# First layer's gathers ordered behind each V block, and the second layer's context projected last

## The chip, the cores and the metric

The kernel runs on one core of one Trainium2 chip. The metric is the device time of one execution in microseconds (us), taken from the first to the last instruction with what lies around them; lower is better. The engines are named as in the profile: PE multiplies matrices, DVE works element by element on tensors, ACT does activations, casts and copies, POOL writes the descriptors of indirect DMAs (the gathers), and SP issues all other DMAs.

## The reference

Two layers over 512 latent tokens (x) and 256 context tokens, 1024 wide, all in float32. Each layer mixes tokens by three head groups and then looks up experts:

```
hx = rmsnorm(x) * (1 + sc1) + sh1                       # the same for the context, hc
ux, uc = split(hx @ w_in), split(hc @ w_in)             # 18 slices of 128 columns
A: conv width 4 -> RG-LRU scan both ways; the context's last state starts x's scan
B: latent attention: x attends to context and x
C: hyena: conv width 3, two long convolutions by FFT
x = x + g1 * (concat(A * gelu, B, C) @ w_out)
hx = rmsnorm(x) * (1 + sc2) + sh2
# PEER: 8 heads, top 16 of 128 x 128 experts: 128 experts a token
x = x + g2 * sum(gate * gelu(hx . u_tab[eid]) * v_tab[eid])
```

The context gets an output of its own only in the first layer. In the second it gives keys, values and the LRU's starting state, so just six of its 18 slices are needed: 0 to 2 (LRU input), 9 and 10 (compressed keys and values) and 11 (rotary key).

## The kernel before, in words

Instructions are written in one stream with a priority for each part (`self.prio(n)`, lower goes first). A scheduler fixes the order of every engine when the program is built, from these priorities and from its own durations. Nothing is reordered at run time: an engine that waits holds up all that stands behind it.

**Experts, first layer.** 384 of the 512 tokens of x are done densely in `peer_x` (L1180): for each of 128 blocks of 128 experts a U block (weights from DRAM, tile `uv`, split into a high half `uvh` on ACT and a low half `uvl` on DVE, then matmuls into `pst`) and a V block (the same split, matmuls into `dacc`). Between them stands `weights` (L1236): it turns the routed gates into dense columns PA and PB by one-hot tiles (`o`, `og`, matmuls `pwt`). This is done in three groups of blocks, 36, 46 and 46 wide; R = 64 U blocks are held at once. The loop over m at L1305 to L1316 writes, for each m, the weights that are due, V block m and U block m + 64.

The last 128 tokens of x and the 256 of the context are done by gathers: 128 indirect DMAs for u and 128 for v per tile of 128 tokens, each one expert row per token (512 KB into one of 5 buffers `grow`), and one DVE multiply-add each (`acc`, L1134 for u, L1147 for v). `gtile_u` and `gtile_v` write them. Before, all of them have priority 6, the dense loop 3, the second layer's front 3 and 4: the scheduler places a gather where it finds DVE free.

**Second layer's front.** `front` norms and transposes x (`ptr`, `hraw`, `hT`), multiplies it by the slices of `w_in` (each split into `w_inh` on ACT and `w_inl` on DVE; matmuls `pwin`), then does hyena (`hpf`, `hpo`), then `lru` for the context (gates `lpg`, `lg`, `lA`, `lT` from `cxx`) and for x (from `xx`) and the keys and values (`bps`). The slices go 12 to 17 (hyena's), 3 to 8, and then the shared ones 9, 10, 11, 0, 1, 2, whose split weights are used for x and for the context (`cT`). `back` loads and splits the eight slices of `w_out` (L577 to L586): five early, three late, and multiplies (`pwo`).

Of the kernel before, what the change touches and what calls it, by code (L numbers as in the profile page):

```python
# [2 lines left out]

# [17 lines left out]
D = 1024  # L21
# [50 lines left out]
class Kern:  # L72
# [101 lines left out]
    def schedule(self):  # L174
        a = self.a
        with ExitStack() as er:
# [28 lines left out]
            with self.prio(6):  # L205
                self.gtile_u(0, gc[0])
                self.gtile_v(0, 1, 0, gc[0])
                self.gtile_u(0, gc[1])
            with self.prio(3):
                gx, ex = self.peer_x(0, 384, 6, 31, 33, (36, 46, 46), ex, rn)  # L210
# [12 lines left out]
            with self.prio(5):  # L223
                gx, _ = self.peer_x(1, 320, 0, 32, 46, (44, 42, 42), (ex,))
            with self.prio(6):
                for i in sorted(gx, reverse=True):
                    self.gtile_u(1, gx[i])
                    self.gtile_v(1, 0, i, gx[i])
# [235 lines left out]
    def front(self, es, ps, pr, l, s, low, side="left", split=True, ctx=False):  # L464
# [26 lines left out]
        with ExitStack() as es2:  # L491
            hp = es2.enter_context(self.pool("hyc" + tg, side=side))
            hc = [hp.tile([128, L], F32, name=f"hc_{i}") for i in range(6)]
            with self.pool("win" + tg, side=side) as sp:

                def post(st, L, j, p):
                    if j < 3:
                        u = sp.tile([128, LX + 3], F32, name="upad", bufs=2)
                        nc.gpsimd.memset(u[:, 0:2], 0.0)
                        nc.gpsimd.memset(u[:, L + 2:L + 3], 0.0)  # L500
                        nc.scalar.copy(u[:, 2:L + 2], p)
                        cw = [self.col(l, "lcw", i * 3 + j) for i in range(4)]
                        self.conv(st["xx"][j], u, L, cw, self.col(l, "lcb", j))
                    elif j < 6:
                        nc.scalar.activation(st["u1"][j - 3], p, AF.Gelu_apprx_tanh)
                    elif j < 9:
                        nc.scalar.copy(st["cq"][j - 6], p)
                    elif j < 11:
                        nc.scalar.copy(st["ckv"][j - 9], p)
                    elif j == 11:  # L510
                        nc.scalar.copy(st["kr"], p[:96])
                    else:
                        u = sp.tile([128, LX + 3], F32, name="upad", bufs=2)
                        nc.gpsimd.memset(u[:, 0:1], 0.0)
                        nc.gpsimd.memset(u[:, L + 1:L + 2], 0.0)
                        nc.scalar.copy(u[:, 1:L + 1], p)
                        cw = [self.col(l, "hcw", i * 6 + j - 12) for i in range(3)]
                        self.conv(hc[j - 12], u, L, cw, self.col(l, "hcb", j - 12))

                def parts(name, L):  # L520
                    return [sp.tile([128, KD, L], F32R if split else F32, name=f"{name}{i}") for i in range(1 + split)]

                hT = parts("hT", L)
# [614 lines left out]
    def gtile_v(self, l, s, t, routed):  # L1138
# [25 lines left out]
        if l == 0:  # L1164
            nc.sync.dma_start(self.sd[s][t], res)
            if s == 0:
                nc.sync.dma_start(self.res[0][:, t, :], self.sd[0][t])
# [298 lines left out]
```

## Time and profile before

| | |
|---|---|
| median of 3 runs | 4270.21 us (4254.28 to 4272.61) |
| profiled execution | 4259.61 us, span 4257.7 us |
| granted PE clock, mean | 0.939 of full |
| busy: PE, DVE, ACT, POOL | 87%, 82%, 45%, 36% |
| dense loop of the first layer, V blocks | 1207.6 to 2456.6 us |
| second layer up to x's first gate | 2456.6 to 2694.05 us |

Busy shares are means over stages with different limits. To see what a moved instruction costs one reads the stage it leaves and the stage it enters: which engine is full there, and which wait ends last. A group's "idle before" is the time for which its engine stood still just ahead of it, and the releaser is what ended that.

### The profile page before, as it was taken

How to read it: one execution, taken by the hardware profiler on the slowest of the kernel's cores; microseconds unless marked ns; L12 is line 12 of the kernel's file. 1: busy time of each engine (PE TensorE's matmuls, PEld its weight loads, DVE VectorE, ACT ScalarE, POOL GpSimd, SP SyncE). 2: the span in 40 equal slices, each digit the busy share in tenths (PEclk: the TensorE clock that was granted, in tenths of full speed). 3: DMA queues.
4: the chain of work that ended last, by engine and by line, in shares of the span. 5: the costliest groups of instructions: out<-in, count | busy, mean ns of one | idle time of the engine just before them, and what ended most of it. 6: DMA issues, size and time to landing. Idle time of an engine off the chain costs nothing.

```text
span 4257.7 us, 63783 instructions
## 1 busy us (share of the span) xinstructions
PE 3709.5 (87%) x22514; PEld 2804.8 (66%) x22514; DVE 3508.1 (82%) x7449; ACT 1902.7 (45%) x3719; POOL 1524.0 (36%) x1225
## 2 busy tenths in 40 slices
PE   6887988967989999988968979888888999999997
PEld 3645544557878878877756656447888877776654
DVE  5746988889899989988898875754898988898988
ACT  4555243523247426622552244633334755555732
POOL 0000345642344564366436620000126345553243
PEclk7998998979989999999989989998999999999999
DMA  6655687885768897799879952242359888888697
GB/s 204 203 178 183 214 307 244 300 288 185 250 226 266 307 363 268 243 361 348 292 233 332 348 181 87 84 142 100 138 180 352 270 296 296 294 299 277 227 352 274
DMA packets 305634, 1063.74 MB, mean 250 GB/s; under 512 B 35756, under 2 KB 42624, under 8 KB 305314
## 3 DMA queue, kind: packets, MB, share of 16 engines
q0 software_dynamic: 165888, 604.05, 40.8%
q1 hardware_dynamic: 139426, 455.61, 30.7%
q8 instruction: 177, 2.90, 0.3%
q14 instruction: 143, 1.17, 0.1%
HBM read 1042.69 MB, written 16.84 MB: 249 GB/s over the span
## 4 chain that ended last, share of the span: by engine, by line
PE 32%; DMA 21%; DVE 19%; issue 16%; POOL 6%; ACT 5%; SPq 0%; POOLq 0%; DVEq 0%; ACTq 0%
PE pst L121 7%; POOL grow L1123 6%; PE dacc L121 6%; DMA grow<-in_peer_u_dram,eid 6%; DMA grow<-in_peer_v_dram,eid 5%; DMA uv<-in_peer_v_dram 4%; PE pwin L121 4%; DMA uv<-in_peer_ut_dram 3%; DVE uvl L114 3%; DVE acc L1147 3%; DVE acc L1134 2%; PE ppq L121 2%; DMA wmod<-in_w_mod_dram 2%; PE pwo L121 1%; PE fp L414 1%
## 5 line engine op out<-in xcount | busy, mean ns | idle before, releaser
L1123 POOL DMA_INDIRECT grow<-in_peer_u_dram,eid x576 | 749.6, 1301 | 1166.6 <-DVE acc L1134 591.8
L1123 POOL DMA_INDIRECT grow<-in_peer_v_dram,eid x576 | 766.8, 1331 | 748.0 <-DVE acc L1147 604.4
L121 PE MATMUL pst<-dhT,uvh 128*128 128x384 f32 (+1 forms) x4096 | 998.6, 328 | 0.0
L113 ACT CAST uvh<-uv 128x1024 fp32r<-128x1024 f32 x491 | 512.9, 1045 | 699.7 <-DMA uv<-in_peer_v_dram 422.4
L121 PE MATMUL pst<-dhT,uvl 128*128 128x384 f32 (+1 forms) x2048 | 695.2, 339 | 115.5 <-DVE uvl L114 83.9
L1147 DVE SCALAR_TENSOR_TENSOR acc<-grow,gate,acc 128x1024 f32<-128x1024 f32 x571 | 732.9, 1283 | 49.9 <-DMA grow<-in_peer_v_dram,eid 42.9
L1134 DVE SCALAR_TENSOR_TENSOR acc<-grow,ghx 128x1024 f32<-128x1024 f32 x576 | 704.4, 1223 | 73.4 <-DMA grow<-in_peer_u_dram,eid 68.4
L121 PEld LDWEIGHTS pst<-dhT,uvh 128*128 128x128 f32 x4096 | 730.6, 192 | 2.8 <-issue 1.2
L114 DVE TENSOR_TENSOR uvl<-uv,uvh 128x1024 fp32r<-128x1024 f32 x491 | 599.5, 1222 | 154.8 <-ACT uvh L113 152.1
L121 PEld LDWEIGHTS pst<-dhT,uvl 128*128 128x128 f32 x2048 | 394.2, 192 | 218.2 <-DVE uvl L114 163.5
L121 PE MATMUL dacc<-uvh,wl 128*128 128x512 f32 x1154 | 482.0, 418 | 40.1 <-ACT uvh L113 21.3
L121 PE MATMUL dacc<-uvl,wh 128*128 128x512 f32 x1154 | 468.8, 406 | 25.7 <-DVE uvl L114 25.4
L121 PE MATMUL dacc<-uvh,wh 128*128 128x512 f32 x1154 | 462.9, 401 | 0.0
L1263 ACT ACTIVATE o<-iota,di2n 128x128 f16<-128x128 f16 x1056 | 325.2, 389 | 27.6 <-PE pwt L1267 27.4
L121 PEld LDWEIGHTS dacc<-uvh,wl 128*128 128x128 f32 x1154 | 220.6, 191 | 130.3 <-ACT uvh L113 37.0
L121 PEld LDWEIGHTS dacc<-uvl,wh 128*128 128x128 f32 x1154 | 221.1, 192 | 84.5 <-DVE uvl L114 40.2
L121 PEld LDWEIGHTS dacc<-uvh,wh 128*128 128x128 f32 x1154 | 221.2, 192 | 47.9
L1267 PEld LDWEIGHTS <-o 128*128 128x128 f16 x4224 | 126.4, 97 | 104.3 <-issue 31.1
L1233 ACT ACTIVATE PA<-pst 128x320 f32<-128x320 f32 (+1 forms) x126 | 58.4, 463 | 290.4 <-PE pst L121 290.3
L1267 PE MATMUL pwt<-og,o 128*128 128x46 f16 (+3 forms) x4224 | 152.3, 183 | 37.1 <-DVE og L1253 29.7
L1233 ACT ACTIVATE PB<-pst 128x384 f32<-128x384 f32 (+1 forms) x130 | 60.0, 462 | 218.2 <-PE pst L121 218.1
L256 POOL MEMSET rmod<- 128x512 f32 (+1 forms) x8 | 3.3, 416 | 421.1 <-PE ptmod L282 171.8
(403 smaller groups left out, 6104.5 us busy)
## 6 DMA issues: line engine op xcount, KB each, us to landing
uv<-in_peer_ut_dram SPq DMA_DIRECT2D x256, 512.0 KB
uv<-in_peer_v_dram SPq DMA_DIRECT2D x256, 512.0 KB
wmod<-in_w_mod_dram SPq DMA_DIRECT2D x96, 512.0 KB
wpq<-in_peer_wq_dram SPq DMA_DIRECT2D x48, 512.0 KB
w_in<-in_w_in_dram SPq DMA_DIRECT2D x72, 256.0 KB
w_in<-in_w_in_dram SPq DMA_DIRECT2D x18, 512.0 KB
grow<-in_peer_u_dram,eid POOLq DMA_INDIRECT x576, 6.6
grow<-in_peer_v_dram,eid POOLq DMA_INDIRECT x576, 6.8
```

Source lines behind the costliest of these rows:

```text
L113: self.nc.scalar.copy(hi, src)
L114: self.nc.vector.tensor_tensor(lo, src, hi.bitcast(F32), op=ALU.subtract)
L121: self.nc.tensor.matmul(p, w[i], x[j], start=start and n == 0, stop=stop and n == len(passes) - 1)
L256: nc.gpsimd.memset(r, 0.0)
L414: self.nc.tensor.matmul(p, w, x, start=(i == 0), stop=(i == len(pairs) - 1))
L1123: self.nc.gpsimd.indirect_dma_start(out=r, out_offset=None, in_=self.a[table], in_offset=bass.IndirectOffsetOnAxis(ap=eid[:, j:j + 1], axi ...
L1134: nc.vector.scalar_tensor_tensor(junk, r, 1.0, hx, op0=ALU.mult, op1=ALU.mult, accum_out=dot[:, j:j + 1])
L1147: nc.vector.scalar_tensor_tensor(acc, r, w[:, j:j + 1], acc, op0=ALU.mult, op1=ALU.add)
L1233: nc.scalar.activation(slot(i), p, AF.Gelu_apprx_tanh)
L1263: nc.scalar.activation(o2[:, q], self.iota, AF.Abs, bias=i2n[:, t, k * NC + q:k * NC + q + 1])
L1267: nc.tensor.matmul(p[:, q, :], o2[:, q, :], og[:, g, q, :], start=(g == 0), stop=(g == 1))
```

## The change

1. `gtile_u` and `gtile_v` become generators that stop after each gather. In the first layer the 384 gathers of x's fourth tile (u, v) and of the second context tile (v) are written in the dense loop with priority 3: `rate` of them behind each step m from 0 on. What is left over is written behind the loop with priority 6. The second layer draws nothing in its loop.
2. The reload of x's fourth tile for the next layer moves from `gtile_v` to behind the loop in `peer_x`.
3. In the second layer's front x is projected alone, in the order 12 to 17, 0, 1, 2, 9, 10, 11, 3 to 8. The context's norm, transposes and six slices come behind hyena, with loads and splits of their own.
4. `back` takes all raw slices of `w_out` of the second layer through one buffer of the early pool.
5. The padded tile `upad` is as long as what it holds.

```diff
-                self.gtile_u(0, gx[3])
-                self.gtile_v(0, 0, 3, gx[3])
-                self.gtile_v(0, 1, 1, gc[1])
+                feed = lambda gx: chain(self.gtile_u(0, gx[3]), self.gtile_v(0, 0, 3, gx[3]), self.gtile_v(0, 1, 1, gc[1]))
+                rest, ex = self.peer_x(0, 384, 6, 31, 33, (36, 46, 46), ex, rn, feed)
...
                 if nA <= m + R < 128:
                     ublock(m + R)
+                for _ in range(self.rate(m, R, widths) if m >= 0 and not half else 0):
+                    next(gathers, None)
...
+                for t in range(nt, 4):
+                    nc.sync.dma_start(self.res[0][:, t, :], self.sd[0][t])
...
+    def rate(self, m, R, widths):
+        if m + R < 128:
+            return 3
+        return 1 if m < 128 - widths[-1] else 2
...
-                shared = (9, 10, 11, 0, 1, 2)
-                order = (3, 4, 5, 6, 7, 8) + shared if ctx else (0, 1, 2, 9, 10, 11, 3, 4, 5, 6, 7, 8)
-                for j in (12, 13, 14, 15, 16, 17) + order:
-                    if ctx and j == shared[0]:
-                        cT = parts("cT", LC)
-                        for _ in self.transposed(sp, ps, l, 0, 1, range(2), cT):
-                            pass
+            with self.pool("win" + tg, side=side) as sp:
+                project(sp, st, s, L, (12, 13, 14, 15, 16, 17, 0, 1, 2, 9, 10, 11, 3, 4, 5, 6, 7, 8), 3)
...
             if ctx:
+                with self.pool("winc", side=side) as sp:
+                    project(sp, sc, 1, LC, (0, 1, 2, 9, 10, 11), 3)
                 kp = ek.enter_context(self.pool("kvc", side="right"))
...
-                    raw = pool.tile([128, D], F32, name="woraw" if l else f"wo{k}")
+                    raw = sp.tile([128, D], F32, name="woraw") if l else pool.tile([128, D], F32, name=f"wo{k}")
```

`project` is the loop over slices that stood in `front`, now for one stream: norm and transposes, then per slice load, split, matmuls and what follows them (`post`).

DVE in the first layer's dense loop, about the 98th streamed block, where the weights of the second group begin. `acc,dot<-grow,ghx` is a gather's multiply-add, `uvl` the low half of a block, PB, PA and `og` are steps of the weights. Before:

```order
L114 TENSOR_TENSOR uvl<-uv,uvh 128x1024
L1134 SCALAR_TENSOR_TENSOR acc,dot<-grow,ghx 128x1024 x3
L1270 SCALAR_TENSOR_TENSOR PB<-pwt,PB 128x28x8
L1270 SCALAR_TENSOR_TENSOR PA<-pwt,PA 128x18x8
L1270 SCALAR_TENSOR_TENSOR PB<-pwt,PB 128x28x8
L1270 SCALAR_TENSOR_TENSOR PA<-pwt,PA 128x18x8
L1253 TENSOR_TENSOR og<-o_14198,diT 128x736
L114 TENSOR_TENSOR uvl<-uv,uvh 128x1024
```

And in the changed kernel, from the same block to the next:

```order
L115 TENSOR_TENSOR uvl<-uv,uvh 128x1024
L1130 SCALAR_TENSOR_TENSOR acc,dot<-grow,ghx 128x1024 x3
L1266 SCALAR_TENSOR_TENSOR PB<-pwt,PB 128x28x8
L1130 SCALAR_TENSOR_TENSOR acc,dot<-grow,ghx 128x1024
L1266 SCALAR_TENSOR_TENSOR PA<-pwt,PA 128x18x8
...
L1130 SCALAR_TENSOR_TENSOR acc,dot<-grow,ghx 128x1024
L1249 TENSOR_TENSOR og<-o_14362,diT 128x736
L1130 SCALAR_TENSOR_TENSOR acc,dot<-grow,ghx 128x1024
L1266 SCALAR_TENSOR_TENSOR PB<-pwt,PB 128x28x8
L1130 SCALAR_TENSOR_TENSOR acc,dot<-grow,ghx 128x1024
L1266 SCALAR_TENSOR_TENSOR PA<-pwt,PA 128x18x8
L115 TENSOR_TENSOR uvl<-uv,uvh 128x1024
```

Nine multiply-adds now stand between two blocks where there were three.

DVE at the end of the dense loop, from the last low half on. `acc<-grow,gate,acc` is a gather's multiply-add for V, `PA<-dacc` reads the dense result, `nrm` and `nry` belong to the second layer's norm. Before:

```order
L114 TENSOR_TENSOR uvl<-uv,uvh 128x1024
L1147 SCALAR_TENSOR_TENSOR acc<-grow,gate,acc 128x1024 x3
L1332 TENSOR_TENSOR PA<-dacc_10668,PA 128x1024
L1332 TENSOR_TENSOR PA<-dacc_10669,PA 128x1024
L1172 TENSOR_TENSOR xs<-PA 128x1024 x2
L1332 TENSOR_TENSOR PA<-dacc_10670,PA 128x1024
L1147 SCALAR_TENSOR_TENSOR acc<-grow,gate,acc 128x1024
L1172 TENSOR_TENSOR xs<-PA 128x1024
L1147 SCALAR_TENSOR_TENSOR acc<-grow,gate,acc 128x1024
L105 TENSOR_SCALAR nrm<-nss 128x1
L1147 SCALAR_TENSOR_TENSOR acc<-grow,gate,acc 128x1024
```

And in the changed kernel:

```order
L115 TENSOR_TENSOR uvl<-uv,uvh 128x1024
L1154 TENSOR_TENSOR acc<-acc,grow 128x1024
L1168 TENSOR_TENSOR grow<-grow,acc 128x1024
L1333 TENSOR_TENSOR PA<-dacc_10668,PA 128x1024
L1333 TENSOR_TENSOR PA<-dacc_10669,PA 128x1024
L1168 TENSOR_TENSOR xs<-PA 128x1024 x2
L1333 TENSOR_TENSOR PA<-dacc_10670,PA 128x1024
L1168 TENSOR_TENSOR xs<-PA 128x1024
L106 TENSOR_SCALAR nrm<-nss 128x1 x2
L107 RECIPROCAL nry<-nry 128x1
```

The multiply-adds behind the last block are gone; the closing sums of the context tile (`acc<-acc,grow`, `grow<-grow,acc`) now stand ahead of the dense result.

ACT in the second layer, around the context's first gates `lg<-lpg`. Before, they stand in hyena (`hab` belongs to hyena), in one run:

```order
L741 ACTIVATE lg_23832<-lpg,sphb 128x256
L746 ACTIVATE lT_23834<-lg_23812,sp_23779 128x256
L748 ACTIVATE lA_23836<-lg_23812,sp_23780 128x256
L746 ACTIVATE lT_23838<-lg_23820,sp_23779 128x256
L748 ACTIVATE lA_23840<-lg_23820,sp_23780 128x256
L746 ACTIVATE lT_23842<-lg_23828,sp_23779 128x256
L748 ACTIVATE lA_23844<-lg_23828,sp_23780 128x256
L752 ACTIVATE lg_23812<-lA_23836 128x256
L752 ACTIVATE lg_23820<-lA_23840 128x256
L650 COPY hab<-hc_22345 128x1
L651 COPY hab<-hc_22345 128x1
L752 ACTIVATE lg_23828<-lA_23844 128x256
```

And in the changed kernel, behind hyena:

```order
L114 CAST w_inh<-w_in 128x512
L500 COPY upad<-pwin 128x256
L114 CAST w_inh<-w_in 128x512 x2
L500 COPY upad<-pwin 128x256
L114 CAST w_inh<-w_in 128x512
L737 ACT_TABLE_LOAD
L737 ACTIVATE lg_23888<-lpg,sphb 128x256
L114 CAST w_inh<-w_in 128x512
L737 ACTIVATE lg_23892<-lpg,sphb 128x256
L737 ACTIVATE lg_23896<-lpg,sphb 128x256
L742 ACTIVATE lT_23910<-lg_23888,sp_23855 128x256
L737 ACTIVATE lg_23900<-lpg,sphb 128x256
```

The gates now stand among the casts of the context's own weight slices (`w_inh`) and the copies of its projections (`upad`); from here to x's first gate ACT has nine table loads.

## Rows read from the trace of the kernel before

**Rows 1.** The page: chain that ended last, shares of the span by engine.

```profile
PE 32%; DMA 21%; DVE 19%; issue 16%; POOL 6%; ACT 5%; SPq 0%; POOLq 0%; DVEq 0%; ACTq 0%
```

**Rows 2.** Windows of the dense stage: length; busy PE, PEld, DVE, ACT, POOL; clock, DMA share.

```profile
1613.80:1799.90 186.10, 184.16 (x1508) 154.23 (x1508) 178.13 (x362) 130.11 (x285) 63.71 (x49) 0.99 0.73 241
1799.90:2082.70 282.80, 253.20 (x1200) 209.09 (x1200) 239.05 (x255) 80.00 (x114) 179.58 (x134) 0.98 0.96 356
2082.70:2227.60 144.90, 110.21 (x1031) 79.20 (x1032) 139.99 (x269) 98.97 (x231) 36.83 (x36) 0.86 0.68 218
```

**Rows 3.** Windows of the seam, the second layer's projection and its hyena.

```profile
2456.60:2493.30 36.70, 8.09 (x33) 6.13 (x32) 36.56 (x60) 21.28 (x50) 14.88 (x17) 0.53 0.84 294
2493.30:2622.20 128.90, 123.12 (x591) 102.74 (x592) 55.54 (x92) 43.42 (x84) 1.57 (x20) 0.96 0.23 73
2622.20:2687.40 65.20, 56.49 (x214) 37.57 (x212) 54.70 (x131) 33.50 (x67) 0.00 (x0) 0.92 0.31 104
```

**Rows 4.** Groups on DVE, 1613.8 to 1799.9: shapes, count | busy us, mean ns | idle before.

```profile
L1134 DVE SCALAR_TENSOR_TENSOR acc<-grow,ghx 128x1024 f32<-128x1024 f32 x49 | 59.9, 1223 | 0.3
```

**Rows 5.** The page's costliest groups: the gathers' multiply-add for V.

```profile
L1147 DVE SCALAR_TENSOR_TENSOR acc<-grow,gate,acc 128x1024 f32<-128x1024 f32 x571 | 732.9, 1283 | 49.9 <-DMA grow<-in_peer_v_dram,eid 42.9
```

**Rows 6.** Groups on DVE in the seam, 2456.6 to 2493.3.

```profile
L1147 DVE SCALAR_TENSOR_TENSOR acc<-grow,gate,acc 128x1024 f32<-128x1024 f32 x16 | 20.4, 1277 | 0.0
```

**Rows 7.** Timeline of SP's DMA queue at the seam: start us, us, instruction.

```profile
2487.23 0.33 SPq L1158 DMA_DIRECT2D grow<-csd  x1
2497.97 0.32 SPq L1165 DMA_DIRECT2D csd<-grow  x1
```

**Rows 8.** Chain that ended last in order of time: start us, us, what.

```profile
2494.87 67.53 PE pwin L121 x287
...
2578.23 8.60 PE pwin L121 x48
...
2694.05 3.04 PE lpg L738 x6
...
2874.52 3.49 DMA woraw<-in_w_out_dram
2880.38 3.61 DMA woraw<-in_w_out_dram
2886.37 35.67 PE pwo L121 x148
```

**Rows 9.** Groups on ACT, 2493.3 to 2694.

```profile
L113 ACT CAST w_inh<-w_in 128x512 fp32r<-128x512 f32 x34 | 21.2, 622 | 27.7 <-PE pwin L121 27.7
L741 ACT ACTIVATE lg<-lpg,sphb 128x256 f32<-128x256 f32 x12 | 5.4, 472 | 5.6 <-PE lpg L738 5.6
L456 ACT ACTIVATE hraw<-ptr,modcol 128x128 f32<-128x128 f32 x12 | 4.9, 466 | 0.1
L748 ACT ACTIVATE lA<-lg,sp 128x256 f32<-128x256 f32 x6 | 3.5, 591 | 0.0
L746 ACT ACTIVATE lT<-lg,sp 128x256 f32<-128x256 f32 x6 | 3.5, 590 | 5.7 <-DVE sp L713 5.7
...
L741 ACT ACT_TABLE_LOAD x2 | 2.6, 1283 | 0.0
...
L113 ACT CAST cT<-hraw 128x512 fp32r<-128x512 f32 x4 | 2.5, 621 | 0.7 <-DVE hraw L454 0.7
L756 ACT ACTIVATE lT<-lT 128x256 f32<-128x256 f32 x6 | 2.4, 417 | 5.1 <-DVE lT L753 5.1
...
L752 ACT ACTIVATE lg<-lA 128x256 f32<-128x256 f32 x6 | 2.1, 403 | 0.0
```

**Rows 10.** Timeline of ACT around a table load.

```profile
2657.00 0.41 ACT L752 ACTIVATE lg<-lA 128x256 f32<-128x256 f32 x1
2657.43 1.28 ACT L756 ACT_TABLE_LOAD   x1
2658.72 0.42 ACT L756 ACTIVATE lT<-lT 128x256 f32<-128x256 f32 x1
```

More of the change, by code (lines that the diff above doesn't have):

```diff
@@ L2 @@
 from contextlib import ExitStack, contextmanager, nullcontext
+from itertools import chain
 import numpy as np
@@ L223, in schedule @@
             with self.prio(5):
[L224 removed]
+                feed = lambda gx: chain(*(g for i in sorted(gx, reverse=True)
+                                          for g in (self.gtile_u(1, gx[i]), self.gtile_v(1, 0, i, gx[i]))))
+                rest, _ = self.peer_x(1, 320, 0, 32, 46, (44, 42, 42), (ex,), feed=feed)
             with self.prio(6):
[L226 to L228 removed]
+                for _ in rest:
+                    pass
     def col(self, l, name, i=0, p=128):
@@ L493, in front @@
             hc = [hp.tile([128, L], F32, name=f"hc_{i}") for i in range(6)]
[L494 to L523, printed above, removed]
@@ new lines, in post @@
+            def post(sp, st, L, j, p):
+                if j < 3:
+                    u = sp.tile([128, L + 3], F32, name="upad", bufs=2)
+                    nc.gpsimd.memset(u[:, 0:2], 0.0)
+                    nc.gpsimd.memset(u[:, L + 2:L + 3], 0.0)
+                    nc.scalar.copy(u[:, 2:L + 2], p)
+                    cw = [self.col(l, "lcw", i * 3 + j) for i in range(4)]
+                    self.conv(st["xx"][j], u, L, cw, self.col(l, "lcb", j))
+                elif j < 6:
+                    nc.scalar.activation(st["u1"][j - 3], p, AF.Gelu_apprx_tanh)
+                elif j < 9:
+                    nc.scalar.copy(st["cq"][j - 6], p)
+                elif j < 11:
+                    nc.scalar.copy(st["ckv"][j - 9], p)
+                elif j == 11:
+                    nc.scalar.copy(st["kr"], p[:96])
+                else:
+                    u = sp.tile([128, L + 3], F32, name="upad", bufs=2)
+                    nc.gpsimd.memset(u[:, 0:1], 0.0)
+                    nc.gpsimd.memset(u[:, L + 1:L + 2], 0.0)
+                    nc.scalar.copy(u[:, 1:L + 1], p)
+                    cw = [self.col(l, "hcw", i * 6 + j - 12) for i in range(3)]
+                    self.conv(hc[j - 12], u, L, cw, self.col(l, "hcb", j - 12))
@@ L524, in front, with project @@
+            def project(sp, st, s, L, order, bufs):
+                hT = [sp.tile([128, KD, L], F32R if split else F32, name=f"hT{i}") for i in range(1 + split)]
                 for _ in self.transposed(sp, ps, l, 0, s, range(L // 128), hT):
                     pass
-                shared = (9, 10, 11, 0, 1, 2)
-                order = (3, 4, 5, 6, 7, 8) + shared if ctx else (0, 1, 2, 9, 10, 11, 3, 4, 5, 6, 7, 8)
-                for j in (12, 13, 14, 15, 16, 17) + order:
-                    if ctx and j == shared[0]:
-                        cT = parts("cT", LC)
-                        for _ in self.transposed(sp, ps, l, 0, 1, range(2), cT):
-                            pass
+                for j in order:
@@ L538, in front @@
                         w = [(raw[:, k, :],) for k in range(KD)]
-                    for n, h, t in ((L, hT, st), (LC, cT, sc)) if ctx and j in shared else ((L, hT, st),):
-                        p = ps.w("pwin")[:, :n]
-                        for k in range(KD):
-                            self.mm([p], [w[k]], [[x[:, k, :] for x in h]], k == 0, k == KD - 1)
-                        post(t, n, j, p)
+                    p = ps.w("pwin")[:, :L]
+                    for k in range(KD):
+                        self.mm([p], [w[k]], [[x[:, k, :] for x in hT]], k == 0, k == KD - 1)
+                    post(sp, st, L, j, p)
+            with self.pool("win" + tg, side=side) as sp:
+                project(sp, st, s, L, (12, 13, 14, 15, 16, 17, 0, 1, 2, 9, 10, 11, 3, 4, 5, 6, 7, 8), 3)
             with self.pool("nrm" + tg, side=side) as sp:
@@ L1304, in peer_x @@
             acc = [pa.S(f"dacc{i}") if i < nd else pa.w(f"dacc{i}") for i in range(nt)]
+            gathers = feed(gx)
             due = {}
```

18 lines of the change are left out of this document (9 added, 9 removed).

## The prediction

> **What bounds the kernel now.** I read the page first, then the stages. The chain that ended last is shared out: PE holds the largest part and DMA, DVE and plain issue follow close behind [rows 1], so no single engine decides and each stage must be read by itself. I therefore asked for the windows of the first layer's dense stage, cut where the change begins and ends to move things [rows 2]. In the first of them, 1613.80 to 1799.90 us (the second group of expert weights is computed there), PE is busy 184.16 of 186.10 us and DVE 178.13, while the DMA share is only 0.73: two engines are full at once. In the second DMA is full (0.96) and DVE has 43.75 us to spare. In the third DVE is the full one, 139.99 of 144.90 us, and PE waits (110.21). The same view of the seam between the layers and of the second layer's front [rows 3] shows a seam of 36.70 us in which DVE is busy 36.56 us and PE 8.09, then a projection of 128.90 us that PE fills (123.12), then 65.20 us of hyena in which PE has 56.49, DVE 54.70 and ACT 33.50: three engines share it. The profiled execution took 4259.61 us, the median of the runs is 4270.21; I make the sum against the first and add it to 4265, half-way between the two.
>
> **The gathers.** The text of the change feeds 302 of the 384 gathers in the dense loop, but the order of DVE moves far fewer. Up to the 98th streamed block, DVE's multiply-adds stand where they stood; behind it nine stand in a row of PB, PA and og steps where there were three; by the end of that weights stage 18 more are done than before; in the next stage the lead falls by 2, in the third it grows by 3, and it ends at 19. Before, these 19 came behind the last V block, mixed into the second layer's first normalisation; now none is left there.
>
> In the first stage one gather is 1.223 us of DVE [rows 4]: 18 x 1.223 = 22.0 us. DVE is idle for 186.10 - 178.13 = 7.97 us of it [rows 2]. If every idle microsecond took a gather the stage would grow by 22.0 - 8.0 = 14.0 us; if DVE kept its present share, 178.13/186.10 = 0.957, it would grow to (178.13 + 22.0)/0.957 = 209.1, by 23.0. What hides gathers elsewhere, PE's own work, hides nothing here, because PE waits for weights and low halves of blocks that DVE makes. In the second stage 2 gathers fewer are worth 0 to -2.6 us (2 x 1.283 [rows 5], DVE is not its bound). In the third, 3 x 1.283 = 3.85 us more fall on a DVE with 4.91 us to spare: 0, or 3.85/0.966 = +4.0 at its present share. Dense stage: +11.4 to +27.0; I take +20, a little over the middle, since both full stages run DVE at 95.7 and 96.6% and never at 100.
>
> At the seam, 16 gathers of the 19 lie inside the 36.70 us and take 20.4 us of DVE [rows 6]. Without them DVE has 36.56 - 20.4 = 16.2 us and ACT, with 21.28 [rows 3], is late next. With some 4 us of start-up in front of ACT the first projection would begin after about 25.7 us: -11. If ACT was paced by DVE all along it could be the whole -20.4; if loads of w_in or the square sums decide, 0.
>
> **The reload and SP's queue.** The reload of x's fourth tile is the same 512 KB in another place. But the context tile's closing DMAs (row, old context, write back) now stand ahead of xs and of the first w_in on SP's queue, where before they came after them. The write back stood 2497.97 - 2487.23 = 10.74 us behind the load of the old context [rows 7], part of that waiting for DVE's last add. w_in and xs are queued behind it now, and the casts and the norm behind these. Between 0 (all done while the last V block multiplies) and +10.7 I take +3, near the lower end, as the last gathers now precede the last block.
>
> **The context projected last.** Before, x and context shared six weight slices. Twelve x-only slices, 287 recorded matmuls, took 67.53 us [rows 8], 5.63 us a slice; a shared one took 8.60, so the context's part of it is 2.97. x alone is 18 x 5.63 = 101.3 us against 128.90 for this stretch [rows 3]: -27.6. Hyena loses the context's gates that filled its gaps; it can't fall below PE's 56.49, so 0 to -8.7; I take -6. Then, between hyena's end and x's first gate, there were about 8 us (2687.4 to 2694.05 and one activation); now the whole context stands there: 16 transposes, 6 slices with weights loaded and split anew, the convolution, gates and both scans. On PE this is 6 x 2.97 = 17.8 us; with the transposed copies in front (4.9 and 2.5 us of ACT [rows 9]) 25 us, if the gates hide behind the slices. On ACT, which now does it alone and not in hyena's gaps, it is 4.9 + 2.5 + 10 casts x 0.622 + 5.4 + 2.1 + 3.5 + 3.5 + 2.4 and, in the new order, nine table loads x 1.283 = 42.0 us, since gates, roots and casts alternate there. Nothing overlapped would be 42 + 25 = 67 us. I take 52: ACT's 42 and 10 for its waits on the first transposes and on DVE. Front: -27.6 - 6 + (52 - 8) = +10.4, between -19.3 and +31.4. The twelve further loads of 256 KB go into a stretch with a DMA share of 0.31, so they cost nothing by themselves; the twelve further subtractions on DVE run beside ACT.
>
> One rule speaks against this part. ACT goes on at once behind a table load: it ends at 2658.71 and the next activation starts at 2658.72 [rows 10]. The Trainium skill, "ScalarE: Activation LUTs", section "What ACT_TABLE_LOAD costs", counts about 1.38 us of drain beside the 1.283 us of the load, 2.66 us a switch. By the rule nine switches would be 23.9 us and not 11.5, the context 12.4 us longer and the whole sum about +30 (4295); the trace has the 1.283 but no drain behind or ahead of it.
>
> **w_out.** Of three late slices of the second layer's output weights one is now loaded early. The last two loads began 5.86 us apart (2874.52, 2880.38) and the output projection took up its work again at 2886.37 [rows 8]: at most -5.9, at least 0 where the remaining two are as late; I take -4.
>
> Sum: 20 - 11 + 3 + 10 - 4 = +18 us, 4265 + 18 = 4283.
>
> **Rivals.** (A) Faster: idle time takes everything. DVE's gaps swallow the gathers (+11.4), the seam gives back all 20.4, the context is done at PE's pace in 25 us (front -19.3), w_out -5.9: -34, 4231. For it speaks that ACT is far from full in hyena and that a seam with PE idle for 28 us is a real hole. Against it: ACT has 42 us of work in one stretch, and DVE never ran above 97%. (B) Slower: the context as a serial chain on ACT, between hyena's end and x's first gate. Its price is 67 us in place of 52, so +33, 4298; it decides from 55 us on, where the sum passes 21 us. For it: its gates need the convolution, which needs the projection, and each direction's square root waits for DVE. Against it: the same work lay in hyena's 65 us and left ACT half idle. The drain rule above would be this rival's second cause. (C) The change does not do what it says: since only 19 gathers move, what they cost in the stage they give back at the seam one for one (+20, -20), and +3 + 10 - 4 = +9 are left, 4274. Against it: ACT stands ready to bound the seam.
>
> **How the numbers follow.** About 0.5% (21 us) is what a measurement of this kernel tells from no change; my forecast lies just inside. Forecast 0.52, with a range of its own of 4270 to 4299 (same 0.30, slower 0.22); A 0.17 (faster 0.15, same 0.02); B 0.20 (slower 0.19, same 0.01); C 0.11 (same 0.08, slower 0.02, faster 0.01). Faster 0.16, same 0.41, slower 0.43. The range of 4256 to 4312 takes in B and C and the half of the way to A that the bounds of the seam and of the context's stretch allow.
>
> **What would show it.** Right: the weights stage of the second group near 206 us with DVE above 95%, the seam near 28 us with ACT busiest, the x projection near 101 us, hyena near 59 and then some 50 us in which PE is less than half busy and ACT full before x's first gate; one wait for woraw less before the output projection. Wrong: a weights stage still near 190 us (A or C), a seam that stays at 36 us with SP or w_in as releaser, or a context stretch of under 35 us or over 60.

## The result, and the profile after

The changed kernel takes 4308.74 us (median of 4 runs, 4304.53 to 4318.35), the kernel before 4271.41 us beside it; the ratio is 1.0094 with a 95% interval of [1.0067, 1.0122]. It is slower by about 40 us (37 between the medians), where +18 had been forecast. The time lies in the predicted range of 4256 to 4312, 3 us below its upper end; the forecast of 4283 was 26 us too low.

The profiled execution of the changed kernel took 4318.35 us (span 4316.6). Set stage by stage against the trace of before it is 58.9 us longer. 7.6 us of this lie where the change touches nothing (6.6 before the first streamed block, -2.4 up to the 98th, 3.4 behind the output projection), so they are the spread between two executions. The rest is 51 us. That is more than the medians differ by and lies at the upper end of the interval (29 to 52 us): the profiled execution of before is 12 us under its median, that of after 10 us above. By stage:

| stage | before | after | difference | predicted |
|---|---|---|---|---|
| weights of the second group | 186.2 | 206.8 | +20.6 | +14 to +23 |
| the stage behind it | 282.8 | 284.0 | +1.1 | -2.6 to 0 |
| weights of the third group | 144.9 | 150.2 | +5.3 | 0 to +4 |
| last V blocks | 229.0 | 229.6 | +0.6 | 0 |
| seam | 36.7 | 25.0 | -11.7 | -11, and +3 for SP |
| projection before hyena | 129.2 | 100.8 | -28.5 | -27.6 |
| hyena | 62.9 | 61.5 | -1.4 | -6 |
| hyena's end to x's first gate | 9.7 | 64.1 | +54.4 | +44 |
| x's first gate to the first scores | 38.6 | 48.6 | +9.9 | 0 |
| first scores to the output projection | 138.4 | 140.8 | +2.4 | 0 |
| output projection | 70.6 | 69.0 | -1.6 | -4 |

Other runs below leave a stage as it is in one of the two kernels, and their traces show how far to trust a row. The weights of the second group take 186.2 to 187.5 us in the four traces with the old order of gathers and 206.6 to 211.9 in the six with the new one; the seam takes 24.9 to 25.0 in these six. From the second layer's first projection slice to the first scores it is 239.6 to 242.2 us in five traces with the shared context pass and 271.7 to 275.6 in four with the pass behind hyena as it stands here.

The windows of the dense stage in the changed kernel, with the columns of [rows 2]:

```profile
1617.90:1824.70 206.80, 187.17 (x1501) 156.98 (x1502) 196.62 (x395) 125.95 (x277) 84.56 (x68) 0.96 0.79 264
1824.70:2108.70 284.00, 258.85 (x1211) 214.56 (x1209) 238.27 (x234) 83.14 (x124) 177.98 (x131) 0.96 0.96 350
2108.70:2258.90 150.20, 110.46 (x1027) 78.04 (x1028) 144.47 (x275) 98.72 (x231) 41.22 (x40) 0.85 0.70 223
```

PE's work in the first row is nearly what it was, 187 us of a longer stage: PE now waits more. DVE works 196.62 us of 206.80, a share of 0.951 as before, only longer. The groups on DVE in that window, beside [rows 4]:

```profile
L1130 DVE SCALAR_TENSOR_TENSOR acc<-grow,ghx 128x1024 f32<-128x1024 f32 x67 | 81.4, 1215 | 1.7 <-DMA grow<-in_peer_u_dram,eid 1.6
```

67 multiply-adds in place of 49 are the 18 that the order showed, 21.5 us of DVE. The nine in a row, behind the 98th block:

```profile
1617.90:1633.40 15.50, 7.01 (x53) 4.97 (x53) 13.74 (x27) 8.10 (x20) 11.46 (x10) 0.82 0.91 324
```

The step from that block to the next takes 15.4 us where it took 6.3, and PE is busy for less than half of it. PE waits there for ACT's high halves (5.5 us), and ACT for blocks from DRAM (10.0 us) at a DMA share of 0.91: in this step the gathers' transfers bear on the time too.

The windows from the seam to the first scores, in the order seam, x's projection, hyena, context, x's gates, beside [rows 3]:

```profile
2488.50:2513.50 25.00, 8.37 (x33) 5.99 (x32) 17.74 (x40) 19.82 (x46) 0.00 (x0) 0.56 0.31 109
2513.50:2614.30 100.80, 100.75 (x432) 82.60 (x432) 43.96 (x68) 31.68 (x54) 0.94 (x14) 0.97 0.26 81
2614.30:2675.80 61.50, 52.61 (x183) 33.43 (x182) 40.05 (x91) 10.62 (x23) 0.00 (x0) 0.89 0.31 103
2675.80:2739.90 64.10, 37.06 (x193) 29.95 (x192) 35.44 (x91) 47.58 (x95) 0.34 (x6) 0.77 0.32 104
2739.90:2788.50 48.60, 34.27 (x77) 15.38 (x77) 30.84 (x52) 36.10 (x59) 0.31 (x1) 0.85 0.13 38
```

DVE's 36.56 us at the seam have become 17.74, and ACT with 19.82 of 25.00 is the fullest. Hyena, without the context's gates, leaves ACT idle for 51 of 61.50 us and is hardly shorter for it (1.4 us). The fourth row is the new stretch: PE busy 37.06 of 64.10, ACT 47.58.

Its first 18 us, on ACT (the number in brackets is the idle time ahead of an instruction and what ended it):

```profile
2677.45 1.06 ACT L422 ACTIVATE xn<-xr 128x1024 f32<-128x1024 f32 x1 [24.98 <-DMA xr<-csd]
...
2683.45 1.86 ACT L457 ACTIVATE hraw<-ptr,modcol 128x128 f32<-128x128 f32 x5 [3.11 <-PE ptr L442]
...
2691.15 1.85 ACT L457 ACTIVATE hraw<-ptr,modcol 128x128 f32<-128x128 f32 x5 [3.11 <-PE ptr L442]
```

ACT stood still for 25 us of hyena with the context's norm at the head of its queue, waiting for the load of the context. SP's queue shows why that load came late:

```profile
2634.62 29.30 SPq L660 DMA_DIRECT2D hkk<-spec  x6
2673.91 0.32 SPq L435 DMA_DIRECT2D xr<-csd  x1
2675.88 5.55 SPq L304 DMA_DIRECT2D w_in<-in_w_in_dram  x5
2682.21 0.33 SPq L435 DMA_DIRECT2D xr<-csd  x1
```

It is issued behind hyena's own loads (`hkk`), 10 us behind the last of them; the second tile's load follows 8 us later, since both go through one buffer. Each tile is a chain of 8 us: load, norm on ACT, DVE's steps, transposes, copies. The first slice of the context starts 17.75 us behind hyena's end; these 17.75 us are called the start-up below.

The context's first slice then runs at the lower level of PE's clock (1.2 GHz, granted clock 0.50), after a stretch in which PE was busy for 4.47 of 18.40 us:

```profile
2694.20:2699.60 5.40, 5.31 (x25) 5.32 (x26) 1.74 (x4) 1.24 (x2) 0.00 (x0) 0.50 0.06 7
```

Its 23 matmuls in one piece take 5.29 us; 20 later ones, at granted clock 1.00, take 2.40 (both in the chain below). About 2.5 us of the stretch are lost by that, an estimate from these two rows.

The chain that ended last, beside [rows 8]:

```profile
2513.55 100.78 PE pwin L122 x432
...
2694.29 5.29 PE pwin L122 x23
...
2715.22 2.40 PE pwin L122 x20
...
2719.17 1.28 ACT L737
2720.96 1.28 ACT L752
2722.93 1.28 ACT L737
...
2741.38 2.90 PE bps L826 x4
2744.28 4.20 PE lpg L734 x6
...
2928.13 3.78 DMA woraw<-in_w_out_dram
...
2934.26 4.33 DMA woraw<-in_w_out_dram
2939.72 37.57 PE pwo L122 x161
```

x alone takes 100.78 us for 18 slices, 5.60 each, as worked out (5.63). Table loads stand on the chain themselves. `bps L826` is the context's values: before, they were done ahead of x's first gate, now they lie among x's gates. That this makes the +9.9 of the table is borne out by a run below in which all of them stand ahead of x's first gate again. The two late loads of `woraw` still stand on the chain, as before.

### The profile page after: what moved, and what is told of

It is laid out like the page before. It is cut to its first block, busy times and chain, and to the rows that moved or that the text cites. A ratio compares the mean times of both kernels' runs of the same rounds, so it can differ in the third digit from the quotient of the medians.

```text
span 4316.6 us, 63859 instructions
## 1 busy us (share of the span) xinstructions
PE 3745.4 (87%) x22514; PEld 2826.9 (65%) x22514; DVE 3520.3 (82%) x7461; ACT 1913.5 (44%) x3735; POOL 1534.3 (36%) x1225
## 4 chain that ended last, share of the span: by engine, by line
PE 34%; DVE 21%; DMA 19%; issue 14%; ACT 6%; POOL 6%; SPq 0%; POOLq 0%; DVEq 0%; ACTq 0%
PE pst L122 9%; POOL grow L1119 6%; PE dacc L122 6%; DMA grow<-in_peer_u_dram,eid 6%; PE pwin L122 4%; DMA grow<-in_peer_v_dram,eid 4%; DMA uv<-in_peer_ut_dram 4%; DMA uv<-in_peer_v_dram 3%; DVE uvl L115 3%; PE ppq L122 3%; DVE acc L1130 3%; DVE acc L1144 2%; PE pwo L122 2%; PE fp L415 1%; ACT uvh L114 1%
## 5 line engine op out<-in xcount | busy, mean ns | idle before, releaser
L1119 POOL DMA_INDIRECT grow<-in_peer_v_dram,eid x576 | 776.1, 1347 | 740.1 <-DVE acc L1144 583.7
L122 PE MATMUL pwin<-hT,w_inh 128*128 128x256 f32 (+1 forms) x672 | 165.3, 337 | 0.1
```

What stands on the lines that cost most here:

```text
L122: self.nc.tensor.matmul(p, w[i], x[j], start=start and n == 0, stop=stop and n == len(passes) - 1)
L1119: self.nc.gpsimd.indirect_dma_start(out=r, out_offset=None, in_=self.a[table], in_offset=bass.IndirectOffsetOnAxis(ap=eid[:, j:j + 1], axi ...
```

## The experiments

Ratios are against the kernel before on the same chip, with their 95% intervals; stage times are from each run's trace.

**Gathers alone** (parts 1 and 2; front and w_out as before).

```diff
+                feed = lambda gx: chain(self.gtile_u(0, gx[3]), self.gtile_v(0, 0, 3, gx[3]), self.gtile_v(0, 1, 1, gc[1]))
+                rest, ex = self.peer_x(0, 384, 6, 31, 33, (36, 46, 46), ex, rn, feed)
...
+                for _ in range(self.rate(m, R, widths) if m >= 0 and not half else 0):
+                    next(gathers, None)
```

> The kernel before with parts 1 and 2 alone (gathers fed in the dense loop, reload moved); the second layer's front and w_out as before. Theory (gathers cost more in the full dense stage than they save at the seam): dense stage about 28 us longer, nearly all of it between the 98th streamed block and the 200th, seam about 12 us shorter, total +16 us (+0.4%). Rival (moved one for one, the whole loss lies in the context): total within 5 us of before. Rival (the gathers make the whole loss): total +40 us.

4281.86 us, ratio 1.0014 [0.9995, 1.0034]: no difference that can be told, -2 to +15 us. In the trace the second group's weights take 210.1 us, the third's 151.2, the seam 24.9, as in the changed kernel, and the second layer is as before. So the stages move as expected and the total less than expected: the theory's +16 lies just above the interval. The rival of the whole loss (+40) is out; the rival that they moved one for one (within 5 us) is not. Set against the trace of w_out alone on the same chip, whose dense stage and seam are as before, these stages together are 13.8 us longer (dense stage +25.6, seam -11.8), which the interval allows.

**Context alone** (parts 3 and 5).

```diff
-                    if ctx and j == shared[0]:
-                        cT = parts("cT", LC)
...
+                with self.pool("winc", side=side) as sp:
+                    project(sp, sc, 1, LC, (0, 1, 2, 9, 10, 11), 3)
```

> The kernel before with part 3 (and 5) alone: context projected behind hyena, gathers and w_out as before. Theory (the context is a serial stretch with a start-up of its own): dense stage and seam unchanged, x's projection 28 us shorter, hyena's end to x's first gate about 64 us in place of 10, the gates of x to the first score matmul 10 us longer, total +35 us (+0.8%). Rival (the context only hurts together with the gathers): total within 10 us of before.

4307.93 us, ratio 1.0070 [1.0049, 1.0092]: +21 to +39 us. Dense stage and seam are as before (187.1 and 35.8), the projection is 101.4, the stretch behind hyena:

```profile
2665.50:2729.80 64.30, 36.97 (x193) 29.52 (x192) 35.56 (x91) 47.88 (x96) 0.34 (x6) 0.73 0.31 103
```

The theory holds. The context makes most of the loss, without the gathers: from the first slice to the first scores 30.4 us more than in the trace of w_out alone, on the same chip.

**w_out alone** (part 4).

```diff
-                    raw = pool.tile([128, D], F32, name="woraw" if l else f"wo{k}")
+                    raw = sp.tile([128, D], F32, name="woraw") if l else pool.tile([128, D], F32, name=f"wo{k}")
```

> The kernel before with part 4 alone: all raw slices of w_out through one buffer, six of eight early. Theory: the output projection takes up its work 2 to 6 us sooner after its first matmuls, total -2 to -6 us, too little for the clock to tell. Rival (the single buffer delays the early loads and so the rest): total +5 us or more.

4275.20 us, ratio 0.9991 [0.9971, 1.0011]. The output projection takes 68.5 us in place of 70.6. As expected, and too little for the timing to tell. It shows in every trace: the projection's matmuls end 47.1 to 48.1 us after their start in the traces with part 4, 49.7 to 51.0 in those without. The ratios of the three parts add up to 0.75%, inside the interval of the whole.

**Gathers held back.** 36 of the context's gathers moved into the second layer's x projection. (The reload of x's fourth tile stands ahead of that tile's last gathers here, so the tile goes into the second layer without its experts.)

```diff
+            if (l, s, t) == (0, 1, 1) and j == n - LATE:          # LATE = 36
+                nc.vector.scalar_tensor_tensor(held, self.hold[:, :128], 0.0, w, op0=ALU.mult, op1=ALU.add)
+                w = held
...
+                    self.hold = hc[0]
+                    for _ in range(LATE // 12 if ctx and j not in shared else 0):
+                        next(late, None)
```

> The kernel before, with the last 36 gathers of the second context tile held back (their weights get a term 0 times the first slice's result, so they can't start earlier) and written three behind each x-only slice of the second layer's projection. Theory (a gather costs what the stage's fullest engine says; in that projection DVE has 73 us to spare and the DMA share is 0.23): seam 12 us shorter, the end of the dense stage 10 to 25 us shorter for 17 to 20 gathers fewer, the projection up to 10 us longer, total -15 to -30 us (-0.4 to -0.7%). Rival (gathers cost DVE time one for one wherever they stand, or PE waits for DVE's low halves of w_in): projection 30 us or more longer, total within 5 us of before or slower.

4296.10 us, ratio 1.0045 [1.0025, 1.0065]: slower, the theory fell. The seam is 26.8 us, but the projection:

```profile
2494.50:2648.50 154.00, 129.08 (x592) 103.84 (x592) 98.22 (x130) 45.39 (x87) 40.07 (x51) 0.93 0.50 174
```

It grew by 25 us though DVE is busy for only 98.22 of 154.00. The waits:

```profile
POOL grow L1132 <- DVE acc L1161: 18.2, 16, 3.2
PE pwin L125 <- DVE w_inl L118: 13.8, 11, 4.7
PE ptr L445 <- DVE xn L427: 9.2, 1, 9.2
```

Two things hold PE up. The low halves of w_in stand behind multiply-adds in DVE's queue, and PE waits 13.8 us for them, in eleven waits. And it waits 9.2 us at once for the context's norm: the held gathers belong to the second context tile, whose result has to be summed, written back and loaded again (3.01 and 3.36 us on the chain) before that norm can begin. So part of the loss is owed to the choice of gathers, not to the place alone. Nor did the last V blocks become faster for 20 gathers fewer (238.2 us against 229.0); why they took 9 us longer stays open.

**Context ahead of hyena**, with loads and splits of its own.

```diff
+            if ctx:
+                with self.pool("winc", side=side) as sp:
+                    project(sp, sc, 1, LC, (0, 1, 2, 9, 10, 11), 3)
             with self.pool("nrm" + tg, side=side) as sp:
```

> The changed kernel, but the context's projection (own loads and splits, as changed) stands ahead of hyena and not behind it. Theory (the loss comes from the place: behind hyena the context is a serial stretch that nothing covers): hyena's end to x's first gate back to about 10 us from 64, hyena's stretch back from 61 to 65 us, projection and context together about 128 us, total about 35 to 45 us less than the changed kernel, that is within 10 us of the kernel before. Rival (the doubled loads, casts and subtractions cost): still 25 us or more above the kernel before.

4303.92 us, ratio 1.0079 [1.0052, 1.0106]. The theory fell for the larger part: from the first projection slice to the first scores it takes 262.0 us against 274.9 in the changed kernel and 240.5 before, so the place behind hyena is worth 13 us and the separate pass 21. The window of the context's pass, now between x's slices and hyena:

```profile
2618.90:2668.20 49.30, 29.44 (x178) 26.68 (x178) 28.97 (x81) 33.47 (x66) 0.13 (x2) 0.76 0.33 102
```

It takes 49.3 us; in the shared pass the context cost 28.5 (129.2 less x's 100.8). 20.4 of them are again the start-up (load, norm and transposes), with PE waiting: the first load is issued only as x's last slice ends, which fits a pool that gets its room then. The rival named the loads and splits; in this window PE waits 3.0 us for low halves and 15.2 for the norm.

**Room on the other side of the memory** for the context's pass behind hyena.

```diff
-                with self.pool("winc", side=side) as sp:
+                with self.pool("winc", side="right") as sp:
```

> The changed kernel with the context's projection in a pool on the other side of the memory, so that its loads need not wait for hyena's room; the order of ACT changes with it, casts first and gates behind all of them, with five table loads ahead of x's first gate in place of nine. Theory (18 us from hyena's end to the context's first matmul are loads and norm that waited for hyena's room, the rest is ACT): the first falls to 5 us or less, and x's first gate comes 15 to 25 us sooner than in the changed kernel. Rival (the start-up is the norm's and the transposes' own length): 18 us stay, gain under 6 us.

4311.74 us, ratio 1.0111 [1.0087, 1.0135]. The start-up is 15.5 us in place of 17.75: the theory fell. Room did hold the load back: SP now issues it at 2659.57, directly behind the last `hkk` and 12 us ahead of hyena's end. But the norm's DVE steps stand behind hyena's last in DVE's queue, so little is won by it; the rival's outcome came, for a reason that it did not name. x's first gate came not sooner but 11 us later (75.0 us behind hyena's end), the casts all going first (seven table loads in the trace, where five had been counted). 10 of these come back in x's gates: 38.5 us, as in the kernel before (38.6), now that all of the context's keys and values stand ahead of x's first gate again.

**Priority**: the context's projection one level ahead of its gates.

```diff
-                with self.pool("winc", side=side) as sp:
+                with self.prio(low - 1), self.pool("winc", side=side) as sp:
```

> The changed kernel with the context's projection one priority level ahead of its gates (casts tend to go ahead of gates on ACT; seven table loads in place of nine; the norm still stands behind hyena's copies). Theory (ACT's order of casts, gates and table loads is 5 us of the stretch, the start-up stays): x's first gate 3 to 8 us sooner than in the changed kernel. Rival (PE or the loads set the stretch): no change within 2 us in the trace.

4309.08 us, ratio 1.0106 [1.0082, 1.0129]. x's first gate stands 68.1 us behind hyena's end, 4 later, x's gates are 5.5 us shorter (six of the twenty matmuls of the context's keys and values stand ahead of them): -1.7 us together. The theory fell; with two table loads fewer nothing is won.

**Another rate**: the nine in a row taken apart.

```diff
         if m + R < 128:
-            return 3
+            return 2 if m < 36 else 4
```

> The changed kernel with two gathers behind V blocks 0 to 35, four behind 36 to 63 and the rest as changed: the nine multiply-adds in a row are gone and DVE's order in the weights stage of the second group is as in the kernel before, with 2 gathers more in place of 18; 14 gathers lie behind the last V block again. Theory (the dense stage grew by the gathers that DVE has to do in a stage where it is full): that stage falls from 206.8 to about 188 us, the dense loop by about 25 us against the changed kernel, the seam grows by 8 to 11, total 10 to 17 us less than the changed kernel. Rival (a gather costs its DVE time wherever it stands): total within 4 us of the changed kernel.

4302.90 us, ratio 1.0090 [1.0067, 1.0114], where the changed kernel has 1.0094; 6 to 9 us under the two runs above on the same chip, which are not the changed kernel. The second group's weights and the seam:

```profile
1613.20:1802.30 189.10, 183.03 (x1505) 153.67 (x1506) 178.47 (x364) 127.33 (x278) 69.89 (x53) 0.99 0.74 247
...
2460.30:2496.10 35.80, 8.08 (x33) 6.13 (x32) 35.66 (x56) 20.00 (x46) 12.80 (x15) 0.55 0.81 279
```

With 2 gathers more in place of 18 the stage is back at 189.1 us with DVE at 178.47, and the seam at 35.8: the theory holds for the stages. Against the trace of the changed kernel the dense loop has 23 us less and the seam 11 more, 13 net. The total does not show it: by the two ratios it is as in the changed kernel, which is the rival's outcome, and their intervals (10 us to each side) allow the theory's 10 as well.

**Context's norm and transposes early**, in x's projection; its slices stay behind hyena.

```diff
+                if ctx:
+                    for _ in self.transposed(sp, ps, l, 0, 1, range(2), cT):
+                        pass
...
-                    project(sp, sc, 1, LC, (0, 1, 2, 9, 10, 11), 3)
+                    project(sp, sc, 1, LC, (0, 1, 2, 9, 10, 11), 3, cT)
```

> The changed kernel, but the context's norm and transposes stand in the second layer's x projection, behind its slices, and their result is kept in a pool of its own; its slices stay behind hyena. ACT has seven table loads from hyena's end to x's first gate in place of nine. Theory (17.8 us from hyena's end to the context's first matmul are its norm and transposes, whose load stands behind hyena's on SP's queue and whose DVE steps stand behind hyena's; the rest of the 64 us is ACT with casts, gates and table loads): the first part falls to 5 us or less, x's projection grows by 0 to 9 us for the transposes, x's first gate comes 8 to 16 us sooner, total -5 to -16 us against the changed kernel. Rival (ACT's work sets the whole stretch and only begins earlier): hyena's end to x's first gate stays above 58 us.

4325.02 us, ratio 1.0101 [1.0081, 1.0120]: no faster than the changed kernel (1.0094). The start-up fell to 5.5 us and x's first gate to 50.1 us behind hyena's end, as the theory said. 9.2 us of it went into the stretch between x's slices and hyena's end, and x's gates took 61.4 us in place of 48.6. There a new wait stands:

```profile
2766.93 0.63 ACT L761 ACTIVATE lT<-lT 128x512 f32<-128x512 f32 x1 [0.32 <-DVE lT L758]
2775.31 1.04 ACT L114 CAST woh<-woraw 128x1024 fp32r<-128x1024 f32 x1 [7.75 <-DMA woraw<-in_w_out_dram]
2781.36 1.05 ACT L114 CAST woh<-woraw 128x1024 fp32r<-128x1024 f32 x1 [5.01 <-DMA woraw<-in_w_out_dram]
```

PE waits 16.3 us for the rotary table in the same place. SP's queue:

```profile
2706.88 1.34 SPq L733 DMA_DIRECT2D gw<-in_lru_g_dram  x1
2771.74 0.33 SPq L586 DMA_DIRECT2D woraw<-in_w_out_dram  x1
...
2772.59 0.42 SPq L795 DMA_DIRECT2D ropep<-in_ropep_dram  x1
```

It issued nothing for 63 us; the pool that keeps the context's transposed tiles stands on the side where these loads go, which fits, though the wait's cause was not tried by itself. So no run shows what the total would be with the start-up covered and nothing else moved.

**Fewer one-hot tiles on DVE**, in the changed kernel.

```diff
-                if i % 2 == 0:
+                if i % 3 == 0:
```

> The changed kernel with one of three wide one-hot tiles o2 made on DVE and two on ACT, in place of one of two each (in both layers). In a weights stage DVE loses 7 or 8 steps of 0.68 us, ACT gets as many rows of eight short activations and one long (about 4 us each). Theory (DVE bounds the weights stages): the second group's stage falls by 4 to 7 us from 206.8 less what the 2 gathers more in it cost, the third's by 3 to 6 us less 5 gathers more, the end of the dense loop falls by 5 us or more. Rival (ACT's casts and PE's waits for them bound these stages as much): no stage falls, those with ACT above 70% grow by 5 to 20 us.

4310.13 us, ratio 1.0060 [1.0039, 1.0082]. The two weights stages:

```profile
1616.20:1818.20 202.00, 189.83 (x1502) 158.34 (x1503) 189.22 (x382) 148.48 (x339) 80.20 (x63) 0.96 0.77 263
2099.40:2253.90 154.50, 112.94 (x1030) 80.87 (x1029) 146.66 (x274) 123.63 (x302) 43.71 (x45) 0.83 0.70 237
```

The first fell by 4.8 us with DVE's load by 7.4: seven o2 tiles fewer on DVE, but also three gathers fewer (64), where two more had been expected. The second grew by 4.3 with 5 gathers more. Dense loop: 873.0 us against 870.6. The second group's stage follows DVE's load; the loop as a whole gained nothing, since the order moved gathers on into the third group's.

**The kernel before with part 4 and fewer one-hot tiles on DVE**, the attempt at a better version, one of three and one of four.

```diff
-                if i % 2 == 0:
+                if i % 3 == 0:
```

In the second run it is `i % 4`.

> The kernel before with part 4 and one of three o2 tiles on DVE: the attempt at a version that beats both kernels. The scheduler, finding DVE freer, places the gathers so that none is left behind the last V block, and 11 more lie in the second group's stage. Theory (DVE bounds the weights stages and the seam): the stage grows by 3 to 9 us (11 gathers are 13.5 us, 7 or 8 o2 tiles less are 5), the seam falls by 11, the second layer's stages fall by 3 to 5 us each, total -5 to -20 us against before. Rival (ACT as in the run with the changed kernel): total +10 us or more.

> As the one before, with one of four o2 tiles on DVE and three on ACT. Theory: DVE loses 4 steps more a stage (2.7 us), ACT gets 16 us more and is above 85% in the third group's stage of the first layer; total within 5 us of the version with one of three. Rival: ACT becomes the bound there and the total is 10 us or more above that version.

4274.38 us, ratio 0.9993 [0.9974, 1.0011], and 4267.34 us, ratio 0.9976 [0.9959, 0.9992]. In the first the seam fell by 12 us (24.7) as expected, but the second group's weights take 197.3 us (+11.1, with 9 gathers more) and the third's 158.3 (+13.4, with 11 more); the theory's -5 to -20 is only in part inside the interval (-11 to +5 us), the rival is out. The second, 7 us under the first by the medians, is the one version here that beats both kernels, by 3 to 18 us against before. What it gained is not located: in its profiled execution (4283.50 us, above its median) the dense loop is 28 us longer than in the trace of before (the third group's weights, where ACT is busy for 133.36 us, take 163.6). Shorter are the seam, 30.4 us, and the stretch behind the output projection, where the second layer's experts have fewer o2 tiles on DVE too: by 8 us against before, the shortest of all traces here, though another run without that edit comes within 5 us of it.

Its second group's weights answer a rival that the runs above leave open. A gather costs a 512 KB transfer as well as DVE time, and the longer stages all had more gathers.

```profile
1620.30:1809.60 189.30, 183.86 (x1508) 154.37 (x1508) 179.05 (x364) 167.69 (x392) 78.50 (x57) 0.99 0.76 263
```

Here 7 gathers more than before stand in the stage (56), and 12 o2 tiles fewer on DVE; DVE's work is 179.05 us where it was 178.13, and the stage is 3 us longer, not the 8 that 7 gathers would cost at the changed kernel's price (20.6 us for 18). So, by this trace, it is DVE's time more than the transfers that lengthens the stage. It is not DVE's time alone: in the version with one of three, DVE's work grew by 5.4 us and the stage by 11.1.

## Why the prediction was right, and what it mis-sized

By its own signs it was right in part. The weights stage (206.8 us, DVE at 0.951), the seam (25.0 us, ACT busiest) and x's projection (100.8) came as it said. But it had named a context stretch of over 60 us as a sign of being wrong, and that stretch is 64.1; PE is busy for 0.58 of it and ACT for 0.74, where "less than half" and "full" had been said. By the traces the sum should have been +51 and was +18. The terms that missed nearly all missed one way: the context by 20 us, the dense stage by 8, hyena by 5, w_out by 2. That the time still fell into the range, 3 us below its end, is owed to the range's width and in part to luck.

*The gathers.* Right, in place and mechanism. The second group's stage grew by 20.6 us (14 to 23 was said), DVE kept its share (0.951 against 0.957), and with 16 of the 18 gathers taken out again the stage returned to 189. The third group's stage took +5.3 where +4.0 was the bound. With +1.1 and +0.6 elsewhere the dense loop grew by 27.7 us, just above my upper bound of 27.0; I had taken 20. The run with the gathers alone cost -2 to +15 us, so as a whole they are a small loss at most. One argument against rival A misread a row: DVE did run above 97%, for 36.56 of the seam's 36.70 us [rows 3].

*The seam.* -11.7 us against -11; ACT is late next, as said.

*SP's queue.* The +3 did not come. In the changed kernel the write back is issued at 2486.66 and w_in at 2489.50, 1 us behind the end of the dense loop; it had been done while the last V block multiplied.

*x's projection.* -28.5 us against -27.6.

*Hyena.* -1.4 us against -6. DVE's and ACT's work went (40.05 and 10.62 us are left), but the length stayed; what holds it, PE's 52.61 us or the chain of its steps, was not tried. PE's 56.49 was no floor, since it held matmuls of the context's gates. Its length goes with the granted clock: hyena had 0.92 before and 0.89 in the changed kernel; in two runs with the same work in it (context alone, another rate) it had 0.94 and took 59.5 and 59.4 us, and in the run with room on the other side, whose loads are issued sooner, 1.00 and 55.8. Which of the two is the cause was not tried.

*The context.* This is the term that was mis-sized. I took 52 us from hyena's end to x's first gate, ACT's 42 and 10 for waits at the start; it is 64.1, and 9.9 more lie among x's gates, which I had at nothing. ACT's own work was 6 us short (47.58 measured). The start was 8 short: 17.75 us and not 10, two tiles in turn through load, norm, transposes and copies, with the load behind hyena's on SP's queue and the norm behind hyena's on DVE's. PE's lower clock behind it, some 2.5 us, was not in the sum. And the context's keys and values were forgotten: before, they were done ahead of x's gates, and with all of them ahead again x's gates took 38.5 us. Together +64.3 against +44. The fault was larger than the place: in the run with the pass ahead of hyena a separate pass still costs 21 us more than the shared one, and its start, with little to cover it, is 20.4 us there. That a covered start would win these back was not shown: the run that covered it lost as much to a later wait.

*w_out.* -1.6 us against -4. The wait that was to go did not: the same two late loads stand on the chain (2928.13 and 2934.26, before 2874.52 and 2880.38). The load that part 4 brings forward, issued at 2857.46 before, was not one of them. Where the 2 us come from stays open.

The rule on table loads did not bear: in the context's stretch ACT's loads are 1.283 us, with 0.1 us idle in all ahead of four of them and 0.1 ahead of three more,

```profile
L737 ACT ACT_TABLE_LOAD x4 | 5.1, 1283 | 0.1
L752 ACT ACT_TABLE_LOAD x3 | 3.8, 1283 | 0.1
```

and in the run with priority two loads fewer won nothing. Rival B (a serial chain on ACT, 67 us, +33) came nearest in size, but it was a chain of loads, norm and transposes first and of ACT second.

## What to carry to other kernels

Work that shares split weights with other work also has its start covered by it: here, in a pass of its own, the context's load, norm and transposes took 17.75 us with no engine busy for much more than half of the time (PE 4.47, DVE 8.58, ACT 9.77 of 18.40 us), and that may be more than the loads and splits that one counts. Work moved off a seam goes into a stage; what it costs there is read from the engine that is full in that stage, whose share does not rise (DVE in the second group's weights: 0.957 before, then 0.951, 0.944 and 0.937 in the runs shown). Order by priority alone does not hold an instruction back: where an engine is planned as free, the scheduler puts it there (of the 302 gathers written into the loop, 19 moved).

## What was not expected of the hardware

A stage with DVE busy for 64% of it (98.22 of 154.00 us) was still lengthened by 25 us by 36 multiply-adds on DVE: 13.8 us of it are PE's waits for low halves that stood behind them in DVE's queue, 9.2 one wait for the result of the held gathers. Taking ACT's table loads from nine to seven, or giving the pass room of its own, moved x's first scores by less than 5 us, counted from the second layer's first slice (273.1 and 270.3 us against 274.9). And a stretch in which PE was busy for 4.47 of 18.40 us cost twice: the first slice behind it ran at granted clock 0.50.
